# A two-block network on one core: diagonals, the values' bias, the state space preparation and weight conversions at other points of the program

## The chip, the cores and the metric

The kernel runs on one core of a Trainium2 chip, in one launch. The metric is the device time in microseconds (us). Five engines work at once, each through its own instructions in order: TensorE (PE in the rows), VectorE (DVE), ScalarE (ACT), GpSimd (POOL) and SyncE (SP), whose instructions here are the issues of transfers (DMA). An instruction waits for others by semaphores.

## The reference, cut to what matters

The network is two blocks of two layers each, on two streams of 256 tokens with 1024 features: the latent stream (LAT, x) and the context stream (CTX). All arithmetic is float32. Block 1:

```
for i in range(2):
    x  = ffn_half(x,  lat_m[0:3], ...)       # both streams: x + 0.5 * gate * swiglu(modulate(rmsnorm(x)))
    xc = ffn_half(xc, ctx_m[0:3], ...)
    h, hc = modulate(rmsnorm(x)), modulate(rmsnorm(xc))
    if i == 0:                               # convolution module, width 31, per channel, both streams
        y, yc = conv_module(h), conv_module(hc)
    else:                                    # neighbourhood attention; the context gives keys and values only
        qkv, qkvc = h @ na_w_qkv + na_b_qkv, hc @ na_w_qkv + na_b_qkv
        y = attention(q, k, v, kc, vc, rpb) @ na_w_o + na_b_o
    x = x + lat_m[5] * y
    x = ffn_half(x, lat_m[6:9], ...)         # and xc in layer 0
```

Block 2 starts from x and from a new context ctx_2; its first layer mixes by attention, its second by a state space scan:

```
a_re, a_im, bb_re, bb_im = s5_discretise(lam_re, lam_im, b_re, b_im, log_step)
y, h_end = s5_scan(u, a_re, a_im, bb_re, bb_im, c_re, c_im, h_re, h_im, emit)   # chunks of 128, two directions
```

The tables that the scan's matrix form needs (powers of a times bb and c, in several layouts) depend on weights alone, not on the streams.

## The kernel before, in words

**Products.** Every float32 product is made of three matmuls over a high part and a low part of each operand (hh and hl of the activations, wh and wl of the weights). Weights are loaded raw by SyncE (`_dma`, L164, three buffers), ScalarE copies the high part wh (L183) and VectorE subtracts to get the low part wl (L188), in `pump`. There are NBUF = 5 converted pieces at a time: when a piece is released, the next is converted.

**Stages.** They are marked f100 (feed-forward), conv, f102 (feed-forward), f110 (feed-forward), na (the neighbourhood attention), f112, and then block 2. A feed-forward stage (`ffn`) makes tiles of 128 hidden features over the 512 tokens of both streams (gu, 48 matmuls; the first n1 = 4 tiles stream by stage, each stream when its norm is ready), and then the down products (pd). Between two stages stands a norm: squares (sq, ScalarE) and their sums (acc, VectorE, L295), a column sum by TensorE (ssq), rv on VectorE (L266), rr on GpSimd (L268), a broadcast by TensorE (bc), then per tile nt (VectorE, L691), hh (ScalarE, L693) and hl (VectorE, L696). The next stage's first products wait for hh and hl.

**The convolution.** pj are the products of the pointwise layer; u comes from them by th and t (ScalarE). Eight channel tiles m follow, most taps on VectorE, some on TensorE by 128x128 diagonal matrices dgw, which ScalarE makes from the identity (L1004).

**The preparation.** `s5_pre` (the task `pre`) works on tables of the state space scan beside the feed-forward stages f100, f102 and f110, for indices d = 0 to 7. For each d GpSimd makes bb and its copy bbz (L2002 to L2007, L2062, L2063), vw (L2073 to L2085) and ow (L2110 to L2120), each twice (r = 1, then 0), and a rotation E in six doublings (L2153 to L2172). TensorE transposes vw (pvt) and multiplies ow with bbz (kp); ScalarE and VectorE copy the results to vt and kt; SyncE moves them through memory (dV, dO, dK, eight loads of tt and a dT, twice, and dE). Its tiles ow, vw, kt and tt have one buffer each. A task is a sequence of small steps; while it is started, one is put into the program whenever TensorE's modelled time has advanced by PRE_STEP. `stop` ends this at a stage's last group, and `drain`, behind f110, puts in all steps that are left.

**The attention's start.** In `na`, products for q, k and v of LAT and then of CTX run (pq, pk, pv); v gets its bias vb when it is copied out of the accumulators (vt, L1246), and vb is loaded in `values` (L1232), once for each group g of columns.

**What sets the order.** The program is written in one sequence, and a scheduler orders each engine's instructions by its own timeline, keeping the dependences. `behind_pe` adds a dependence without a wait, which holds an instruction behind the last matmul written so far in this order. On the chip each engine, SyncE too, goes through its instructions in the order so found.

Of the kernel before, what the change touches and what calls it, by code (L numbers as in the profile page):

```python
# [7 lines left out]
F32 = mybir.dt.float32  # L8
F32R = mybir.dt.float32r
AF = mybir.ActivationFunctionType  # L10
# [4 lines left out]
KT = 8  # L15
T = 256
FGROUPS = [(0, 6), (6, 8), (14, 8)]
NBUF = 5
# [59 lines left out]
class Core:  # L78
    def __init__(self, ctx, tc, ap):
        self.tc, self.nc, self.ap, self.es = tc, tc.nc, ap, ctx  # L80
        nc = tc.nc
        self.pe_t = 0.0
        self.n_mm, self.marks, self.pin = 0, [], None
        self.chains = []
        self.ticking = False
        self.tasks = []
        self.cv_behind = None
        P = lambda name, bufs, **kw: ctx.enter_context(tc.tile_pool(name=name, bufs=bufs, **kw))
        self.pool = lambda name, bufs=1, side="left": tc.tile_pool(name=name, bufs=bufs, side=side, reuse_waits="tile")
        self.const = P("const", 1)  # L90
        self.rawp = P("raw", NRAW)
        self.wp = P("w", NBUF)
        self.xp = P("xres", 1)
        self.hp = P("h", 1)
        self.sm = P("small", 3)
        self.tp = P("tmp", 3)
        self.psm = P("psm", 5, space=PSUM)
        self.psa = P("psa", 3, space=PSUM)
        self.chunks, self.pieces = [], []
        self.n_dma = self.n_cv = self.n_take = self.n_rel = 0  # L100
        self.dma_max, self.dma_behind = 1 << 30, False
        self.raw_t, self.cv_t, self.low_p = {}, {}, None

    def mark(self, name):
# [63 lines left out]
        self.n_dma += 1  # L168

    def pump(self):  # L170
        while self.n_cv < min(len(self.pieces), self.n_rel + NBUF):
            ci, off, n = self.pieces[self.n_cv]
            if ci >= self.dma_max:
                return
            while self.n_dma < min(len(self.chunks), ci + 1):
                self._dma()
            nc = self.nc
            r = self.raw_t[ci][:, off * 128:(off + n) * 128]
            hi = self.wp.tile([128, 8, 128], F32R, tag="wh", name="wh")
            lo = self.wp.tile([128, 8, 128], F32R, tag="wl", name="wl")  # L180
            h2 = hi[:, :n, :].rearrange("p k m -> p (k m)")
            l2 = lo[:, :n, :].rearrange("p k m -> p (k m)")
            ins = nc.scalar.activation(out=h2, in_=r, func=AF.Copy)  # L183
            if self.cv_behind:
                self.behind(ins, self.cv_behind)
            eng = nc.gpsimd if self.cv_behind else nc.vector
            self.low()
            self.low_p = lambda eng=eng, l2=l2, r=r, h2=h2: eng.tensor_sub(l2, r, h2.bitcast(F32))  # L188
            self.cv_t[self.n_cv] = (hi, lo)
            self.n_cv += 1  # L190
            last = self.n_cv == len(self.pieces) or self.pieces[self.n_cv][0] != ci
            if last:
                self.raw_t.pop(ci)
            while self.n_dma < min(len(self.chunks), ci + NRAW, self.dma_max):
                self._dma()
# [276 lines left out]
class Net(Core):  # L472
# [24 lines left out]

    def load_x(self, s, name):
        t = self.xp.tile([128, KT, T], F32, tag=f"x{s}", name=f"x{s}")
        self.nc.sync.dma_start(out=t, in_=self.ap[name])  # L500
        self.x[s] = t


    def load_c(self, names):
# [213 lines left out]
    def ffn(self, b, streams, ready, gate, after, nsplit=4, first=1, work=None, side=None, head=0, tail=0, begin=None):  # L718
# [5 lines left out]
        with ExitStack() as es:  # L724
# [12 lines left out]

            def background():
                nonlocal task
                if side is not None and not side.done:  # L740
                    self.start(side)
                if work is None:
                    return
                gen, n = work() if callable(work) else work
                task = Task(self, gen, (0.84 if two else 0.8) * (342e3 if two else 171e3) / n)
                self.start(task)
# [4 lines left out]
            def gu(ws, f0, c0, n, last=True, outer=None):  # L751
                glu(products(ws, c0, n, last, outer), f0, c0, n)
# [58 lines left out]
            for g, (f0, nf) in enumerate(FGROUPS):  # L811
                f = 0
                lastg = g == len(FGROUPS) - 1
                while f < nf:
                    if g == 0 and f == 0:
                        n1 = head + 2 if head else first
                        ws = {}
                        if begin:
                            with self.pool("room") as rp, tc.manual_schedule():
                                begin = begin([[rp.tile([128, 512], F32, name=f"room{i}{k}") for k in range(8)] for i in range(2)])  # L820
                                next(begin)
                                ws = [(self.take(), self.take()) for _ in range(first)]
                                ps = products(ws, 0, N, step=begin)
                                next(begin, None)
                            rooms()
                            glu(ps, 0, 0, N)
                            background()
                        for s in () if begin else streams:
                            order = list(range(n1)) if s == streams[0] else list(range(head, n1)) + list(range(head))
                            self.force(ready[s])  # L830
                            if not head:
                                ws = ws or [(self.take(), self.take()) for _ in range(first)]
                                gu(ws, 0, s * T, T, s == streams[-1])
                                continue
                            for i in order:
                                if i not in ws:
                                    ws[i] = (self.take(), self.take())
                                gu([ws[i]], i, s * T, T, s != streams[0] or i < head, i == order[0])
                                if i < head:
                                    ws.pop(i)  # L840
                        f += n1
                    else:
                        gu([(self.take(), self.take())], f, 0, N)
                        f += 1
                full = KT - nsplit if (lastg and two) else KT
# [115 lines left out]
    def conv(self, ready, gate, after, NPE=8, L=1, n_last=14):  # L961
# [3 lines left out]
        with self.pool("conv") as cp:  # L965
# [23 lines left out]
            def taps(m, ss, n_pe=NPE):  # L989
# [11 lines left out]
                dgs = diag.setdefault(m, [])  # L1001
                while len(dgs) < len(ek):
                    dg = cp.tile([128, 128], F32, tag="dgw", name="dgw", bufs=20)
                    nc.scalar.activation(out=dg, in_=self.ident, func=AF.Copy, scale=w(ek[len(dgs)]))  # L1004
                    dgs.append(dg)
                for i, k in enumerate(dk[2:]):
                    o = (vm, b2)[i % 2]
# [165 lines left out]
    def na(self, ready, gate, after, NR=1.1, NL=0.2):  # L1173
        nc, tc = self.nc, self.tc
        with self.pool("na") as np_, self.pool("na2", 2) as n2:
# [48 lines left out]
            new = lambda name: self.psm.tile([128, 512], F32, tag="m", name=name)  # L1224
            o_rhs = lambda k: self.h_rhs(k, 0, T)

            def produce():

                def values(g, ws, ts):
                    if g not in vb:  # L1230
                        vb[g] = n2.tile([128, T], F32, tag="vb", name="vb", bufs=1)
                        nc.sync.dma_start(out=vb[g], in_=self.ap["vbias"][g * T:(g + 1) * T].partition_broadcast(128))  # L1232
                        v_[g] = [n2.tile([128, 4, T], F32R, tag=f"v{x}", name=f"v{x}") for x in "hl"]
                    vh, vl = v_[g]
                    for t in ts:
                        ps = new("pv")
                        for k in range(KT):
                            wh, wl = [w.rearrange("p k m -> p (k m)")[:, (k % 4) * T:(k % 4 + 1) * T] for w in ws[k // 4]]
                            xh, xl = self.h_rhs(k, t * 128, 128)
                            self.mm(ps[:, :T], xh, wh, k == 0, False, 109)  # L1240
                            self.mm(ps[:, :T], xh, wl, False, False, 109)
                            self.mm(ps[:, :T], xl, wh, False, k == KT - 1, 109)
                            if k == 3:
                                yield
                        tmp = self.tp.tile([128, T], F32, tag="nt", name="vt")
                        nc.vector.tensor_add(tmp, ps[:, :T], vb[g])  # L1246
                        nc.scalar.activation(out=vh[:, t, :], in_=tmp, func=AF.Copy)
                        nc.vector.tensor_sub(vl[:, t, :], tmp, vh[:, t, :].bitcast(F32))
                        if t == 3:
                            vt[g] = (vh, vl)  # L1250
                        yield
# [5 lines left out]
                        yield  # L1257
                    q_out(m, ps)

                vb, v_ = {}, {}  # L1260

                wq, wk, *ws = [self.take() for _ in range(4)]
                wq1 = self.take()
# [51 lines left out]
                while done["pv"] < 16:  # L1315
                    yield
                split_o(7)
                for d, (w, ps) in enumerate(part):
                    self.gemm(ps[:, :T], w, o_rhs, [(7, 7)], False, True)
                    out(d, ps)  # L1320
                    self.release(1)
# [1110 lines left out]
    def network(self, out):  # L2432
# [79 lines left out]
        self.mark("na")  # L2512
        self.na(ready, gates(1, 1, 1, (LAT,)), lambda s, acc: norm(1, 1, 2, s, acc))

        self.load_x(CTX, "ctx_2")

        def ctx_norm():
            acc = self.new_acc(CTX)
# [89 lines left out]
```

## Time and profile before

| | us |
|---|---|
| median of 3 runs | 3609.77 (3609.4 to 3611.73) |
| profiled execution | 3612.36 |
| its span | 3610.5 |
| TensorE busy | 3482.7 |
| VectorE busy | 2590.3 |
| ScalarE busy | 1389.1 |
| GpSimd busy | 749.8 |

Matmuls overlap, and their ends are modelled, so busy time is not time at the peak. "Idle before" is the time an engine stood still just before an instruction, and behind the arrow stands what ended it. A stage's worth is read at its borders, where the engine at the end of the chain waits.

### The profile page before, as it was taken

What the parts mean: (1) busy time and instruction counts of PE and PEld (TensorE: products, weight loads), DVE (VectorE), ACT (ScalarE), POOL (GpSimd) and SP (SyncE); (2) the same over time, 40 slices, a digit from 0 to 9 for tenths busy, and PEclk for the clock granted to TensorE, in tenths of its full rate; (3) what the DMA queues carried; (4) which work ended last, traced back from release to release, by engine and by line L of the source; (5) the groups of instructions that cost most, each with busy time, mean ns of one, the idle gap of its engine ahead of it and who ended that gap; (6) DMA issues with size and microseconds to landing.
All of it is one profiled execution on the core that took longest, in us unless ns stands there. A gap on an engine that the chain in (4) does not pass through costs nothing.

```text
span 3610.5 us, 54700 instructions
## 1 busy us (share of the span) xinstructions
PE 3482.7 (96%) x21248; PEld 3056.4 (85%) x21248; DVE 2590.3 (72%) x4487; ACT 1389.1 (38%) x2428; POOL 749.8 (21%) x870
## 2 busy tenths in 40 slices
PE   8999998999999999999999999889999999999898
PEld 7888867888898888989998889779888988897898
DVE  8987697876586765768987766878887633368655
ACT  4222444422242323554443234655322432244443
POOL 5100001577657772000000001211000100014000
PEclk9999999999999999999999999999999999999899
DMA  7555211455454774236755542014557332238353
GB/s 260 200 189 197 71 59 48 162 190 186 164 169 170 257 242 138 92 120 235 262 187 188 182 145 97 34 50 153 208 206 247 134 124 94 102 120 300 121 197 119
DMA packets 157835, 579.35 MB, mean 160 GB/s; under 512 B 25220, under 2 KB 56708, under 8 KB 117896
## 3 DMA queue, kind: packets, MB, share of 16 engines
q1 hardware_dynamic: 157576, 575.86, 45.8%
q8 instruction: 167, 2.74, 0.3%
q14 instruction: 92, 0.75, 0.1%
HBM read 546.50 MB, written 29.29 MB: 159 GB/s over the span
## 4 chain that ended last, share of the span: by engine, by line
PE 89%; DVE 7%; ACT 2%; issue 1%; POOL 1%; DMA 0%; SPq 0%; POOLq 0%; DVEq 0%; ACTq 0%
PE gu L109 46%; PE pd L109 24%; PE pj L109 8%; PE po L109 2%; PE ptap L109 1%; PE pv L109 1%; PE pk L109 1%; PE ps L109 1%; DVE wl L188 1%; PE ssq L109 1%; PE pT L109 1%; PE pq L109 1%; PE bc L109 1%; DVE ry L2291 0%; DVE jk L612 0%
## 5 line engine op out<-in xcount | busy, mean ns | idle before, releaser
L183 ACT ACTIVATE wh<-raw 128x1024 fp32r<-128x1024 f32 (+1 forms) x679 | 700.8, 1038 | 1581.4 <-PE gu L109 911.7
L188 DVE TENSOR_TENSOR wl<-raw,wh 128x1024 fp32r<-128x1024 f32 (+1 forms) x677 | 839.3, 1244 | 358.5 <-ACT wh L183 348.2
L109 PE MATMUL gu<-hl,wh 128*128 128x512 f32 (+1 forms) x3136 | 1083.8, 347 | 5.6 <-DVE hl L696 4.6
L109 PE MATMUL gu<-hh,wh 128*128 128x512 f32 (+1 forms) x3136 | 1076.9, 348 | 10.0 <-ACT hh L693 6.2
L109 PE MATMUL gu<-hh,wl 128*128 128x512 f32 (+1 forms) x3136 | 1082.0, 346 | 0.0
L538 DVE CUSTOM_DVE_ANT_0 jk<-mw,cb,vec 128x1024 bf16<-128x1024 f32 x480 | 639.0, 1331 | 73.2 <-DMA mw<-in_mw_dram 68.4
L109 PEld LDWEIGHTS gu<-hl,wh 128*128 128x128 f32 x3136 | 600.7, 192 | 78.2 <-DVE hl L696 6.0
L109 PEld LDWEIGHTS gu<-hh,wh 128*128 128x128 f32 x3136 | 596.9, 192 | 81.6 <-ACT hh L693 7.6
L109 PEld LDWEIGHTS gu<-hh,wl 128*128 128x128 f32 x3136 | 600.7, 192 | 70.3 <-issue 1.0
L109 PE MATMUL pd<-Hl,wh 128*128 128x256 f32 (+1 forms) x1696 | 561.8, 332 | 0.0
L109 PE MATMUL pd<-Hh,wl 128*128 128x256 f32 (+1 forms) x1696 | 561.0, 332 | 0.0
L109 PE MATMUL pd<-Hh,wh 128*128 128x256 f32 (+1 forms) x1696 | 559.0, 331 | 0.0
L268 POOL TENSOR_TENSOR rr<-rv,mhalf 128x2 f32<-128x2 f32 (+1 forms) x34 | 28.9, 850 | 1852.9 <-DVE rv L266 1796.4
L109 PEld LDWEIGHTS pd<-Hl,wh 128*128 128x128 f32 x1696 | 322.0, 190 | 30.2 <-issue 0.4
L109 PEld LDWEIGHTS pd<-Hh,wl 128*128 128x128 f32 x1696 | 321.9, 190 | 30.2 <-issue 0.4
L109 PEld LDWEIGHTS pd<-Hh,wh 128*128 128x128 f32 x1696 | 321.5, 190 | 29.9
L779 DVE TENSOR_TENSOR gu<-sg,gu 128x512 f32<-128x512 f32 (+1 forms) x196 | 113.4, 579 | 192.6 <-PE gu L109 191.6
L109 PE MATMUL pj<-hh,wh 128*128 128x256 f32 (+1 forms) x736 | 226.3, 322 | 15.4 <-ACT hh L693 9.0
L109 PE MATMUL pj<-hl,wh 128*128 128x256 f32 (+1 forms) x736 | 231.2, 318 | 1.1 <-DVE hl L1089 1.0
L109 PE MATMUL pj<-hh,wl 128*128 128x256 f32 (+1 forms) x736 | 228.5, 316 | 1.1 <-DVE wl L188 1.1
L109 PEld LDWEIGHTS pj<-hh,wh 128*128 128x128 f32 x736 | 142.0, 200 | 25.8 <-ACT hh L693 9.9
L109 PEld LDWEIGHTS pj<-hl,wh 128*128 128x128 f32 x736 | 146.8, 200 | 9.0 <-issue 1.7
(425 smaller groups left out, 4332.1 us busy)
## 6 DMA issues: line engine op xcount, KB each, us to landing
raw<-in_gu_dram SPq DMA_DIRECT2D x186, 1024.0 KB, 4.9
mw<-in_mw_dram SPq DMA_DIRECT2D x280, 512.0 KB, 4.6
raw<-in_dn2b_dram SPq DMA_DIRECT2D x38, 1024.0 KB, 4.7
raw<-in_dn1b_dram SPq DMA_DIRECT2D x32, 1024.0 KB, 5.3
raw<-in_dn1a_dram SPq DMA_DIRECT2D x16, 768.0 KB, 4.4
raw<-in_pw_dram SPq DMA_DIRECT2D x12, 1024.0 KB, 4.7
raw<-in_dn2a_dram SPq DMA_DIRECT2D x16, 768.0 KB, 4.3
dO<-ow SPq DMA_DIRECT2D x32, 256.0 KB, 2.6
```

The lines of the kernel that those rows point to most:

```text
L109: ins = self.last_mm = self.nc.tensor.matmul(out=out, lhsT=lhsT, rhs=rhs, start=start, stop=stop, **kw)
L183: ins = nc.scalar.activation(out=h2, in_=r, func=AF.Copy)
L188: self.low_p = lambda eng=eng, l2=l2, r=r, h2=h2: eng.tensor_sub(l2, r, h2.bitcast(F32))
L268: nc.gpsimd.tensor_tensor(r[:, :ncol], v[:, :ncol], self.mhalf[:, :ncol], ALU.pow)
L538: self.behind_pe(nc.vector.tensor_tensor_reduce(out=jk, in0=tl[i], in1=self.cb[s], scale=1.0, scalar=self.V(f"mod_b{b}{l}")[:, j:j + 1], o ...
L779: nc.vector.tensor_mul(pr[:, :n], sg[:, :n], pu[:, :n])
```

## The change

Four things stand at other points of the program; no operation is added or removed.

- The diagonals dgw (now L1009) are held behind the last matmul written so far, by `behind_pe`.
- The preparation goes on in f102 and f110 not at the stage's start but at the second tile after the first n1 tiles. In f100 it starts as before.
- The load of the first vb is written at the head of `na`, ahead of the products, and the load of x for block 2's context (L500) is held behind the last matmul written so far.
- At the end of `na` a limit `cv_max` lets `pump` convert only what is left for the output projection and two pieces of f112, until f112's first norm is ready.

```
     def pump(self):
-        while self.n_cv < min(len(self.pieces), self.n_rel + NBUF):
+        while self.n_cv < min(len(self.pieces), self.n_rel + NBUF, self.cv_max):
...
             def background():
                 nonlocal task
-                if side is not None and not side.done:
+                if begin is not None and not side.done:
                     self.start(side)
...
                             self.force(ready[s])
+                            if self.cv_max < 1 << 30:
+                                self.cv_max = 1 << 30
+                                self.pump()
...
                     else:
+                        if g == 0 and f == n1 + 1 and side is not None and not side.done and side not in self.tasks:
+                            self.start(side)
                         gu([(self.take(), self.take())], f, 0, N)
...
-                    nc.scalar.activation(out=dg, in_=self.ident, func=AF.Copy, scale=w(ek[len(dgs)]))
+                    self.behind_pe(nc.scalar.activation(out=dg, in_=self.ident, func=AF.Copy, scale=w(ek[len(dgs)])))
...
+            vb = {}
+
+            def vbias(g):
+                vb[g] = n2.tile([128, T], F32, tag="vb", name="vb", bufs=1)
+                nc.sync.dma_start(out=vb[g], in_=self.ap["vbias"][g * T:(g + 1) * T].partition_broadcast(128))
+            vbias(0)
...
                 split_o(7)
+                self.cv_max = self.n_take + KT - 3 + 2
...
-        self.load_x(CTX, "ctx_2")
+        self.behind_pe(self.load_x(CTX, "ctx_2"))
```

The rows of the order below name tiles without their numbers where one is like another; numbers that stay tell buffers apart.

On ScalarE at the convolution's start, before (hh_96 to hh_100 are the tiles hh3 to hh7 of LAT):

```order
153 L693 ACTIVATE hh_95<-nt,mod_212 128x256
154 L285 ACTIVATE sq<-x_225 128x256
155 L183 ACTIVATE wh<-raw 128x1024
156 L1004 ACTIVATE dgw<-cst,vec 128x128 x17
157 L285 ACTIVATE sq<-x_225 128x256
158 L693 ACTIVATE hh_96<-nt,mod_212 128x256
159 L1004 ACTIVATE dgw<-cst,vec 128x128
160 L693 ACTIVATE hh_97<-nt,mod_212 128x256
161 L1004 ACTIVATE dgw<-cst,vec 128x128 x2
162 L693 ACTIVATE hh_98<-nt,mod_212 128x256
```

and after, from the same place, up to the first dgw:

```order
155 L183 ACTIVATE wh<-raw 128x1024
156 L285 ACTIVATE sq<-x_225 128x256
157 L693 ACTIVATE hh_96<-nt,mod_212 128x256
158 L693 ACTIVATE hh_97<-nt,mod_212 128x256
159 L693 ACTIVATE hh_98<-nt,mod_212 128x256
...
169 L693 ACTIVATE hh_99<-nt,mod_213 128x256
170 L985 ACTIVATE th<-pj,hb_3373 128x256
171 L693 ACTIVATE hh_100<-nt,mod_213 128x256
172 L1009 ACTIVATE dgw<-cst,vec 128x128 x8
173 L183 ACTIVATE wh<-raw 128x1024
```

The 20 dgw among the hh of LAT are gone from there; eight stand behind the last hh of CTX.

On GpSimd at the attention's start, before: the end of the last rotation E, and then rr of LAT, of CTX and of later norms in one row of six:

```order
651 L2166 TENSOR_TENSOR pt_11687<-E_12267 128x8x31
652 L2167 TENSOR_TENSOR E_12266<-pt_11686,pt_11687 128x8x31
653 L2170 TENSOR_TENSOR pt_11686<-E_12266,E_12267 128x8x31
654 L2171 TENSOR_TENSOR pt_11687<-E_12267,E_12266 128x8x31
655 L2172 TENSOR_TENSOR E_12267<-pt_11686,pt_11687 128x8x31
656 L268 TENSOR_TENSOR rr<-rv,mhalf 128x2 x6
```

and after, the stretch that ends with rr of CTX (ow_12576 and ow_12577 are ow of index 7, r = 0; E_12601 and E_12602 its rotation):

```order
611 L2127 TENSOR_TENSOR ow_12576<-ow_12576,ow_12578 128x576
612 L2166 MEMSET E_12601 128x8
613 L2169 COPY E_12601<-cc_1001 128x8
614 L2098 TENSOR_TENSOR vw_12554<-vw_12554,vw_12555 128x512
615 L2131 TENSOR_TENSOR ow_12578<-pw_12455,bc 128x576
616 L2178 TENSOR_TENSOR pt_12457<-E_12601 128x8
617 L2133 TENSOR_TENSOR ow_12577<-ow_12577,ow_12578 128x576
618 L2167 MEMSET E_12602 128x8
619 L2169 COPY E_12602<-cs_1002 128x8
620 L268 TENSOR_TENSOR rr<-rv,mhalf 128x2
621 L2179 TENSOR_TENSOR pt_12458<-E_12602 128x8
622 L2180 TENSOR_TENSOR E_12601<-pt_12457,pt_12458 128x8
```

The rr of LAT stands 84 instructions ahead of this one, and between them are the ow of index 6 (r = 0), its rotation E, and bb, bbz, both vw and both ow of index 7.

On SyncE up to the first vb, before (in front of these stand the four dE of index 7):

```order
390 L164 DMA raw<-in_naqk_dram 128x2048
391 L164 DMA raw<-in_nav_dram 128x2048
392 L2199 DMA dK_166<-kt 128x240
393 L2021 DMA tt<-dK_166 16x4x128 x8
394 L2023 DMA dT_174<-tt 128x512
395 L2021 DMA tt<-dK_166 16x4x128 x8
396 L164 DMA raw<-in_naqk_dram 128x2048
397 L2023 DMA dT_174<-tt 128x512
398 L500 DMA x_15165<-in_ctx_dram 128x2048
399 L1232 DMA vb<-in_vbias_dram 128x256
```

and after:

```order
367 L2212 DMA dK_166<-kt 128x240
368 L2034 DMA tt<-dK_166 16x4x128 x8
369 L2036 DMA dT_174<-tt 128x512
370 L2034 DMA tt<-dK_166 16x4x128 x6
371 L2193 DMA dE_157<-E_12601 128x256
372 L2193 DMA dE_158<-E_12601 128x256
373 L2034 DMA tt<-dK_166 16x4x128 x2
374 L2193 DMA dE_157<-E_12602 128x256
375 L2193 DMA dE_158<-E_12602 128x256
376 L2036 DMA dT_174<-tt 128x512
377 L164 DMA raw<-in_naqk_dram 128x2048
378 L1236 DMA vb<-in_vbias_dram 128x256
```

The load of x is gone from in front of vb, and the dE of index 7 have come in front of it.

## Rows read from the trace of the kernel before

**Rows 1.** The page, part 4: chain that ended last, by engine.

```profile
PE 89%; DVE 7%; ACT 2%; issue 1%; POOL 1%; DMA 0%; SPq 0%; POOLq 0%; DVEq 0%; ACTq 0%
```

**Rows 2.** Stretches: busy us of PE, PEld, DVE, ACT, POOL; granted clock; DMA; GB/s.

```profile
400.00:420.00 20.00, 15.70 (x114) 15.10 (x113) 15.77 (x36) 14.79 (x40) 0.70 (x1) 0.91 0.26 97
640.00:660.00 20.00, 13.36 (x75) 12.65 (x75) 19.79 (x26) 11.38 (x21) 16.69 (x18) 0.70 0.39 116
1040.00:1060.00 20.00, 18.00 (x143) 17.80 (x142) 20.00 (x25) 9.61 (x19) 18.41 (x11) 0.94 0.73 223
1620.00:1640.00 20.00, 13.11 (x82) 12.52 (x81) 15.41 (x33) 10.99 (x23) 0.70 (x1) 0.74 0.55 205
...
440.00:560.00 120.00, 120.00 (x487) 84.84 (x487) 117.24 (x182) 44.38 (x94) 0.00 (x0) 1.00 0.13 46
1412.40:1441.40 29.00, 22.25 (x180) 21.39 (x176) 18.48 (x42) 11.05 (x22) 0.87 (x1) 0.98 0.57 177
```

**Rows 3.** Timeline at the convolution's start: start, duration, engine, instruction [idle before].

```profile
406.02 5.07 ACT L1004 ACTIVATE dgw<-cst,vec 128x128 f32<-128x128 f32 x17
...
411.85 0.39 PE L109 MATMUL pj<-hh,wh 128*128 128x256 f32 x1 [4.25 <-ACT hh L693]
```

**Rows 4.** Timeline at f102's start, PE and DVE; last an hl elsewhere.

```profile
643.37 0.58 PE L109 MATMUL gu<-hl,wh 128*128 128x256 f32 x1 [2.51 <-DVE hl L696]
...
646.45 2.59 DVE L696 SCALAR_TENSOR_TENSOR hl<-nt,mod,hh 128x256 fp32r<-128x256 f32 x2
...
655.92 0.77 PE L109 MATMUL ssq<-invd,acc 128*128 128x1 f32 x3 [3.17 <-DVE acc L295]
...
1419.34 0.87 DVE L696 SCALAR_TENSOR_TENSOR hl<-nt,mod,hh 128x256 fp32r<-128x256 f32 x2
```

**Rows 5.** Group by line on GpSimd: busy, mean ns | idle before.

```profile
L2110 POOL TENSOR_TENSOR ow<-pw,bc 128x576 f32<-128x576 f32 x16 | 24.3, 1520 | 99.7 <-PE kp L109 99.5
```

**Rows 6.** Timeline of GpSimd, index 7 up to the norms.

```profile
1312.30 0.40 POOL L2002 TENSOR_TENSOR pt<-bc,cfr 128x128 f32<-128x128 f32 x1
...
1326.77 2.27 POOL L2085 TENSOR_TENSOR vw<-vw,vw 128x512 f32<-128x512 f32 x1
...
1345.25 1.06 POOL L2073 TENSOR_TENSOR vw<-pw,bb 128x512 f32<-128x512 f32 x1 [1.71 <-PE pvt L109]
...
1351.66 1.29 POOL L2085 TENSOR_TENSOR vw<-vw,vw 128x512 f32<-128x512 f32 x1
1362.21 1.17 POOL L2110 TENSOR_TENSOR ow<-pw,bc 128x576 f32<-128x576 f32 x1 [9.26 <-PE kp L109]
...
1367.23 2.29 POOL L2120 TENSOR_TENSOR ow<-ow,ow 128x576 f32<-128x576 f32 x1
1375.96 0.12 POOL L2153 MEMSET E<- 128x8 f32 x1 [6.45 <-PE pvt L109]
...
1395.21 0.79 POOL L2172 TENSOR_TENSOR E<-pt,pt 128x248 f32<-128x248 f32 x1
...
1419.50 0.87 POOL L268 TENSOR_TENSOR rr<-rv,mhalf 128x2 f32<-128x2 f32 x1 [13.72 <-DVE rv L266]
```

**Rows 7.** Timeline of TensorE at the attention's start.

```profile
1411.79 0.67 PE L109 MATMUL kp<-ow,bbz 128*32 128x128 f32 x16
...
1422.52 0.60 PE L109 MATMUL bc<-cst,rr 128*128 128x128 f32 x4
```

**Rows 8.** Timeline there: SyncE's queue (SPq), VectorE, TensorE.

```profile
1432.91 0.42 SPq L1232 DMA_DIRECT2D vb<-in_vbias_dram  x1
...
1440.98 0.42 DVE L1246 TENSOR_TENSOR vt<-pv,vb 128x256 f32<-128x256 f32 x1 [2.62 <-DMA vb<-in_vbias_dram]
...
1441.46 0.58 PE L109 MATMUL pv<-wh,hh 128*128 128x256 f32 x1 [5.10 <-DVE vt L1246]
```

**Rows 9.** Timeline at f112's start: VectorE and TensorE.

```profile
1614.35 1.22 DVE L188 TENSOR_TENSOR wl<-raw,wh 128x1024 fp32r<-128x1024 f32 x1 [3.04 <-ACT wh L183]
...
1629.04 1.02 PE L109 MATMUL ssq<-invd,acc 128*128 128x1 f32 x4 [4.75 <-DVE acc L295]
```

More of the change, by code (lines that the diff above doesn't have):

```diff
@@ L100, in __init__ @@
         self.n_dma = self.n_cv = self.n_take = self.n_rel = 0
-        self.dma_max, self.dma_behind = 1 << 30, False
+        self.dma_max, self.dma_behind, self.cv_max = 1 << 30, False, 1 << 30
         self.raw_t, self.cv_t, self.low_p = {}, {}, None
@@ L499, in load_x @@
         t = self.xp.tile([128, KT, T], F32, tag=f"x{s}", name=f"x{s}")
-        self.nc.sync.dma_start(out=t, in_=self.ap[name])
         self.x[s] = t
+        return self.nc.sync.dma_start(out=t, in_=self.ap[name])
     def load_c(self, names):
@@ L1230, in values @@
                     if g not in vb:
-                        vb[g] = n2.tile([128, T], F32, tag="vb", name="vb", bufs=1)
-                        nc.sync.dma_start(out=vb[g], in_=self.ap["vbias"][g * T:(g + 1) * T].partition_broadcast(128))
+                        vbias(g)
+                    if g not in v_:
                         v_[g] = [n2.tile([128, 4, T], F32R, tag=f"v{x}", name=f"v{x}") for x in "hl"]
@@ L1258, in query @@
                     q_out(m, ps)
-                vb, v_ = {}, {}
+                v_ = {}
                 wq, wk, *ws = [self.take() for _ in range(4)]
```

## The prediction

> **What bounds the kernel now.** I read the page's chain first, then the stretches at the stage borders, then single instructions there. TensorE carries 89% of the chain that ended last, VectorE 7%, GpSimd 1% [rows 1]. Outside the borders there is next to nothing to win, so every part of the change is priced at the border that it touches. Five borders matter, and each is a different wait [rows 2]: the convolution's start (TensorE busy 15.70 of 20 us), the start of f102 (13.36 of 20, granted clock 0.70), the start of f110 (18.00), the attention's start (22.25 of 29) and the start of f112 (13.11 of 20, clock 0.74).
>
> **Part 1, the diagonals.** Before the convolution ScalarE makes 17 dgw in a row, 5.07 us, between hh2 and hh3, and TensorE's first pj after them waits 4.25 us for hh [rows 3]. In the new order hh3 to hh7 and the next stream's hh go first, and 8 dgw follow. The tap stage behind it is VectorE's (117.24 of 120 us busy, ScalarE 44.38 [rows 2]): an earlier start moves it forward whole, and the dgw, made in ScalarE's gaps, are covered. I take the 4.25 us and 1.25 of the 1.8 us that the clock of 0.91 costs in those 20 us: minus 5.5. Bounds: 0, if VectorE's taps start by something else, and minus 6.0.
>
> **Part 2, the state space preparation's new start.** At f102's start GpSimd works 16.69 of 20 us [rows 2], and VectorE's operations beside it are longer: two hl took 2.59 us there and 0.87 where GpSimd was quiet [rows 4]. TensorE waits for those hl and for an acc: 2.51 and 3.17 us in the two large gaps [rows 4]. With GpSimd quiet, most of the stretch's 6.64 idle us goes, and part of what its clock of 0.70 costs [rows 2]: minus 7.5, bounds minus 2 (the acc chain stays late by itself) and minus 9. At f110's start the same reading gives the 2.00 idle us: minus 2, bounds 0 and minus 2.
>
> What is moved must still be done. The two later starts put the whole train (GpSimd, TensorE's pvt and kp, the copies, SyncE's dV, dO, dK, tt, dT, dE) back by five tiles each (n1 + 1). A tile is 48 matmuls over 512 columns, which I take as 96 over 256; 180 matmuls of the kernel's usual sort take 22.25 us [rows 2], so five tiles are some 59 us, twice. The train can't catch up: its buffers are single, and in front of GpSimd's ow alone it already stands idle for TensorE for 99.7 us in all [rows 5]. After f110 the program drains what is left. Before, that was one kp: it stands behind the last pd and ends at 1412.46 (call this K), and GpSimd had finished its last rotation at 1396.0 [rows 6, 7]. In the new order the kp behind the last pd is of index 6, so on GpSimd the rest of 6 and all of 7 stand behind K, and the second stream's rr stands behind all of that but the last rotation: 84 operations between the two rr, where there were none.
>
> The price by rows 6, as they ran for index 7 before:
> - three ow groups of five, 1362.21 to 1369.52 = 7.31 each: 21.9; two single ow products at 1.17: 2.3
> - one rotation E, 1375.96 to 1396.0: 20.0
> - bb, bbz and the first vw, 1312.30 to 1329.04 = 16.7, less two ow products in it (2.3): 14.4
> - the second vw group, 1345.25 to 1352.95 = 7.7, and one more product of 1.06: 8.8
>
> Sum 67.4 us as they ran. Some of these were held: the same vw addition took 2.27 us and 1.29 [rows 6]. My estimate is one such excess for each ow group, two for each vw, some 4 us in the bb stretch and 5 in the rotation: 12 in all, and 55 for the quiet chain. While it runs VectorE has little to do, since its next rv and hl wait for this very chain; so I stand near the quiet end, 58, and add 2 for the handovers to TensorE and back: rr at K+60 (bounds 55 and 69), against 1419.50 = K+7 before [rows 6]. TensorE's work of the first stream is over long before: from K to 1441.40 it had only 22.25 us of work for both streams [rows 2].
>
> The Trainium skill, "SBUF — State Buffer", section "Who interferes with whom", says that GpSimd and a VectorE instruction with two SBUF inputs exclude each other for whole instructions. The 2.59 against 0.87 us of rows 4 agree that one is held. By that rule a drain beside an idle VectorE would run at the 55 us end, and the total would come out 3 us lower; by the rows as they ran 9 higher.
>
> **Part 3, the values' bias.** Before, SyncE issues vb at 1432.91, right behind the load of x, VectorE's vt begins at 1440.98, and TensorE gets on at 1441.46 = K+29 after 5.10 us [rows 8]. The load of x now stands elsewhere, which alone would save that wait. But vb is still behind the last dT, and now behind the last dE too, and SyncE issues in order: dE needs the rotation E of index 7, which follows the rr. So: rr at K+60; the rest of that rotation 15.5 (bounds 14 and 18, from the 20.0 without its first operations, and without held ones); four issues of about 0.4 (vb's own 0.42): 1.6; landing and vt 7 (before 8.07, from 1432.91 to 1440.98; 3 at least, since there is no load of x ahead); 0.5 from vt to TensorE. TensorE resumes at K+84.6, where it resumed at K+29.0: **plus 55.6**, bounds plus 45 (55+14+1.6+3+0.5 = K+74) and plus 68 (K+97). What hides it: only those 22.25 us, used up on both sides. From rr to the second stream's bc took 3.0 us [rows 6, 7], and the 13.8 us of products between that bc and the wait (1422.52 to 1441.46, less 5.10) then end by about K+77, so vb is the last wait, if not by much. Behind the stalled TensorE stand the weight conversions, for lack of buffers; nothing in the attention gives the time back.
>
> **Part 4, the limit on conversions.** At f112's start ssq waits 4.75 us for acc [rows 9]; VectorE works through weight conversions of 1.22 us between the adds [rows 9], three fewer now (3.7 us). They come back while TensorE works on the first tiles. Minus 3 with the clock (0.74); bounds 0 (ScalarE's part or the adds set it) and minus 5.
>
> **Sum.** -5.5 - 7.5 - 2 - 3 + 55.6 = +37.6 us. The profiled execution took 3612.36 us, so 3650.0; it is 2.6 above the median of 3609.77 of the timed runs, so I predict 3647. Bounds: +45 - 22 = +23 and +68 - 2 = +66, that is 3633 to 3676.
>
> **Rivals.**
> (a) The drain is hidden, and it ends faster: GpSimd comes to the border with less behind K than the order suggests, or its operations run ahead of TensorE. For it: GpSimd has 1% of the chain before [rows 1]. Against: it waits for TensorE's kp and pvt by its single buffers [rows 5], and the order puts rr behind them. It decides from where TensorE resumes at K+47 (29 + 18); wholly hidden it gives 3610 - 18 = 3592.
> (b) The same stall, but GpSimd's operations run as long as in rows 6 (67 and 18), and the borders give back little: +68 - 8 = +60, 3670. For it: VectorE still copies kt and converts weights meanwhile; against: rows 4 show operations held only where both are busy.
> (c) vb isn't the last wait, since its small loads land quickly: then TensorE is late by the rr alone, K+63 at bc against 1422.52 = K+10, 53 us, less the 5.10 that vb cost before: 48 - 18 = +30, 3640.
>
> **How the numbers follow.** The forecast has 0.60, (b) 0.13, (c) 0.14, (a) 0.13, of which 0.09 full and 0.03 about even. A measurement of this kernel can tell 0.2%, 7 us, from no change. Slower by more than that: the forecast, (b), (c) and a rest of (a), 0.88; within it 0.03; faster 0.09. The range leaves out (a) and the far end of (b): 3622 to 3668; the likeliest case's own is 3635 to 3660.
>
> **What would show it.** After: pj without the 4.25 us gap at the convolution's start; VectorE's hl at f102's start at about 0.43 us each; rr of the attention's second stream some 50 us or more behind the first, with rotations and ow, vw between; TensorE nearly idle for over 50 us before the second stream's products; vb issued right behind dE and dT. I am wrong if the two rr stand within 25 us of each other, or if the attention's start is no longer than before.

## The result and the profile after

The changed kernel takes 3634.82 us (median of 4 runs, 3632.36 to 3639.12), the kernel before 3609.76; the ratio is 1.0068, with an interval of 1.0056 to 1.0081. It is slower by 25 us, where 37 were forecast (3647, range 3622 to 3668). The profiled execution took 3634.27 us, its span is 3632.5. That is 22 us above the profiled execution before (3612.36), which ran 2.6 us over its median; so the traces show 22 us where the timed medians show 25.

The chain that ended last, by engine, answers to [rows 1]:

```profile
PE 86%; DVE 7%; POOL 3%; issue 2%; ACT 1%; DMA 0%; SPq 0%; POOLq 0%; DVEq 0%; ACTq 0%
```

GpSimd's share has grown from 1% to 3%. The stretches show where. They answer to [rows 2], with the same columns, and each window is moved about as far as the first rr of its stage moved (the table below has these shifts). The fourth runs from the end of the kp behind the last pd to the end of the stall, the fifth is the start of f112:

```profile
400.00:420.00 20.00, 18.43 (x128) 17.34 (x127) 16.91 (x40) 10.75 (x22) 0.73 (x2) 0.91 0.25 100
638.00:658.00 20.00, 18.90 (x146) 18.90 (x146) 17.92 (x37) 13.34 (x26) 1.54 (x1) 0.91 0.50 186
1026.00:1046.00 20.00, 20.00 (x169) 20.00 (x169) 20.00 (x35) 11.13 (x22) 8.87 (x5) 1.00 0.56 185
1391.50:1473.00 81.50, 39.78 (x275) 34.79 (x273) 25.62 (x46) 15.83 (x32) 69.26 (x120) 0.68 0.41 127
1648.80:1668.80 20.00, 13.09 (x83) 12.51 (x82) 15.46 (x34) 11.04 (x23) 0.71 (x1) 0.74 0.68 259
```

The start of f102 is nearly full now (18.90 of 20, before 13.36) and that of f110 full (20.00, before 18.00); f112's is as it was (13.09, before 13.11). At f102's start GpSimd works 1.54 us, and the two hl that took 2.59 us there [rows 4] take 0.89:

```profile
640.87 0.89 DVE L696 SCALAR_TENSOR_TENSOR hl<-nt,mod,hh 128x256 fp32r<-128x256 f32 x2
```

The attention's start has become a stretch of 81.5 us in which GpSimd works 69.26 and TensorE 39.78; TensorE's granted clock in it is 0.68.

GpSimd in that stretch (start, duration, instruction, idle before), from the first stream's rr to the second's and to the end of the last rotation; this answers to [rows 6]:

```profile
1384.14 0.71 POOL L268 TENSOR_TENSOR rr<-rv,mhalf 128x2 f32<-128x2 f32 x1 [26.87 <-DVE rv L266]
1391.66 1.68 POOL L2123 TENSOR_TENSOR ow<-pw,bc 128x576 f32<-128x576 f32 x1 [6.81 <-PE kp L109]
...
1446.40 1.41 POOL L2133 TENSOR_TENSOR ow<-ow,ow 128x576 f32<-128x576 f32 x1
...
1448.13 0.71 POOL L268 TENSOR_TENSOR rr<-rv,mhalf 128x2 f32<-128x2 f32 x1
...
1464.10 0.72 POOL L2185 TENSOR_TENSOR E<-pt,pt 128x248 f32<-128x248 f32 x1
```

The two rr are 64.0 us apart (before 14.4), and the second waits for nothing but the instructions in front of it: no bracket stands behind it. From the first ow on GpSimd nowhere pauses for more than 0.14 us, so the drain is GpSimd's own work and waits for no other engine. Before, GpSimd had waited 13.72 us for the second rr's input [rows 6].

TensorE there, answering to [rows 7, 8]:

```profile
1390.87 0.67 PE L109 MATMUL kp<-ow,bbz 128*32 128x128 f32 x16
...
1432.48 1.11 PE L109 MATMUL pvt<-cst,vw 128*128 128x128 f32 x4 [24.24 <-POOL vw L2090]
...
1445.22 1.11 PE L109 MATMUL pvt<-cst,vw 128*128 128x128 f32 x4 [4.89 <-POOL vw L2098]
...
1451.23 0.58 PE L109 MATMUL pk<-hh,wh 128*128 128x256 f32 x1 [1.11 <-ACT hh L693]
...
1463.79 0.36 PE L109 MATMUL pv<-wh,hh 128*128 128x256 f32 x1 [2.85 <-DVE kl L1202]
...
1473.00 0.79 PE L109 MATMUL pk<-hh,wh 128*128 128x512 f32 x1 [5.00 <-DVE vt L1258]
```

K, the end of the kp, is at 1391.54, 20.9 us earlier than before. TensorE then meets the preparation's transposes, which wait for GpSimd's vw, and resumes for good at 1473.00 = K+81.5, where it resumed at K+29.0. Its last transposes get their vw only at 1445.22, 2.9 us before the second rr. So two things hold the second stream's products back: the rr in GpSimd's queue, and these transposes, which stand in front of the products in TensorE's own order. No run here moves the rr alone. SyncE's queue and VectorE give the last wait:

```profile
1464.85 0.81 SPq L2193 DMA_DIRECT2D dE<-E  x2
1465.83 0.33 SPq L2036 DMA_DIRECT2D dT<-tt  x1
1466.20 0.44 SPq L164 DMA_DIRECT2D raw<-in_naqk_dram  x1
1466.69 0.44 SPq L1236 DMA_DIRECT2D vb<-in_vbias_dram  x1
...
1472.52 0.42 DVE L1258 TENSOR_TENSOR vt<-pv,vb 128x256 f32<-128x256 f32 x1 [8.88 <-DMA vb<-in_vbias_dram]
```

The last dE goes out when the rotation has ended (1464.82), and vb behind it.

Each norm has its rr on GpSimd, in the same sequence in every kernel, and these serve as milestones. The table gives how much later each comes than in the profile before (us, minus is earlier), for the changed kernel and for the experiments below. "First" and "second" are the two streams; the second rr of f102 lies behind both large gaps of [rows 4]; "end" is the last rr, at 3600.3 before.

| kernel | f102, first (630.7) | f102, second (658.5) | f110, first (1022.1) | attention, first (1405.1) | attention, second (1419.5) | f112 (1630.3) | 2492.9 | end |
|---|---|---|---|---|---|---|---|---|
| changed | -2.0 | -10.7 | -14.1 | -20.9 | +28.6 | +28.8 | +29.7 | +21.9 |
| 1 late only | +1.4 | -7.1 | -10.7 | -17.5 | +32.0 | +32.7 | +33.2 | +25.0 |
| 2 without late | -3.7 | -4.8 | -3.1 | -1.4 | -1.4 | -0.8 | +1.9 | -6.7 |
| 3 all, 1200 | -1.7 | -10.4 | -10.9 | -10.3 | -10.3 | -12.0 | -10.2 | -16.0 |
| 4 late in f110 | +0.6 | +0.6 | +0.6 | -3.8 | +5.4 | +10.3 | +11.7 | +7.0 |
| 5 limit only | -1.6 | -1.6 | -2.8 | +1.1 | +1.1 | -2.4 | -2.9 | -3.8 |
| 6 diagonals only | -2.6 | -3.8 | -2.0 | -1.4 | -1.4 | -4.5 | -6.2 | -16.0 |
| 7 bias and x only | +0.1 | +0.1 | +0.1 | +0.1 | +0.1 | -0.9 | -0.9 | -7.3 |
| 8 all, vb elsewhere | -1.7 | -10.4 | -13.9 | -20.7 | +28.8 | +24.7 | +26.9 | +21.4 |
| 9 1200 only | +0.7 | +0.7 | +2.2 | +5.8 | +5.0 | +3.9 | +3.7 | -4.5 |
| 10 late, 1200 | +1.0 | -7.6 | -8.3 | -7.2 | -7.2 | -9.2 | -7.7 | -13.2 |
| 11 all, 1250 | -3.5 | -12.0 | -8.1 | -12.5 | -9.5 | -6.2 | -4.7 | -9.9 |

So the 22 us of the profile are: 20.9 won up to the attention, 49.7 lost between there and f112, and 6.9 won behind it, in block 2.

### The profile page after: what moved, and what is told of

It reads as the page before. It is cut to its first block, busy times and chain, and to the rows that moved or that the text cites. A ratio compares the mean times of both kernels' runs of the same rounds, so it can differ in the third digit from the quotient of the medians.

```text
span 3632.5 us, 54687 instructions
## 1 busy us (share of the span) xinstructions
PE 3481.5 (96%) x21248; PEld 3053.3 (84%) x21248; DVE 2570.5 (71%) x4487; ACT 1387.4 (38%) x2428; POOL 730.9 (20%) x870
## 4 chain that ended last, share of the span: by engine, by line
PE 86%; DVE 7%; POOL 3%; issue 2%; ACT 1%; DMA 0%; SPq 0%; POOLq 0%; DVEq 0%; ACTq 0%
PE gu L109 46%; PE pd L109 23%; PE pj L109 8%; PE po L109 2%; PE ptap L109 1%; PE pk L109 1%; PE ps L109 1%; PE pv L109 1%; DVE wl L188 1%; PE ssq L109 1%; PE pT L109 1%; PE bc L109 1%; PE pq L109 0%; DVE tl L1601 0%; DVE ry L2304 0%
```

## The experiments

Theory A: the tail of the preparation, pushed behind f110, makes the whole loss. Rivals are named in the expectations. All times are medians, ratios are to runs of the kernel before on the same chip.

**1. Part 2 alone** on the kernel before:

```
-                if side is not None and not side.done:
+                if begin is not None and not side.done:
...
+                        if g == 0 and f == n1 + 1 and side is not None and not side.done and side not in self.tasks:
+                            self.start(side)
```

> Only part 2 on the kernel before (the state space preparation goes on later in f102 and f110); diagonals, bias, x and conversions as before. Theory A (the preparation's tail stands behind f110 and in front of the attention's second rr): 3637 us (3625 to 3645), and the two rr of the attention's start some 60 us apart. Rival B (the loss comes from the moved loads of vb and x or from the limit on conversions, and the later start costs nothing): 3590 to 3600 us, rr 15 us apart.

Measured 3637.51 us, ratio 1.0074 (1.0057 to 1.0091). Part 2 alone makes the loss, and the rr of the attention are 64 us apart (14.4 before, and 49.5 more by the table). Rival B falls.

**2. Parts 1, 3 and 4 without part 2.**

```
-                        if g == 0 and f == n1 + 1 and side is not None and not side.done and side not in self.tasks:
-                            self.start(side)
...
-                if begin is not None and not side.done:
+                if side is not None and not side.done:
```

> Parts 1, 3 and 4 without part 2. Theory A: no stall; the 5.1 us wait for vb goes and the convolution starts 2 to 5 us earlier: 3597 to 3604 us. Rival B: the attention's start stays long: 3625 us or more. Rival C (small shifts of order in block 2 are worth as much as the parts): anywhere in 3595 to 3612, with the differences behind f112.

Measured 3603.84 us, ratio 0.9982 (0.9973 to 0.9992): 6 us faster than before. But at f112 it is level (-0.8), and the gain stands in block 2. Of these parts only the load of x reaches into block 2, and the gain there is no smaller in experiment 6, which leaves that load alone. A's stall is gone, but the 6 us are of C's kind.

**3. The whole change with closer steps.**

```
-PRE_STEP = 1500
+PRE_STEP = 1200
```

> The whole change, with PRE_STEP 1200 in place of 1500: the preparation's steps come closer together, and by the order of GpSimd none stands between or behind the two rr of the attention. Theory A (the tail alone makes the loss; the earlier arrival at the attention, 20.9 us, is mostly quiet borders): 3580 to 3595 us. Rival D (the 20.9 us are mostly work that was pushed out of f102 and f110 into the stall, and comes back when it is done there): 3597 to 3606 us. Rival B: 3625 us or more.

Measured 3593.87 us, ratio 0.9953 (0.9938 to 0.9968). With no instruction of the preparation left between or behind the two rr, 41 us of the changed kernel's time are gone, and it beats both kernels. GpSimd's rr and the resuming TensorE in it:

```profile
1394.73 0.71 POOL L268 TENSOR_TENSOR rr<-rv,mhalf 128x2 f32<-128x2 f32 x1 [8.24 <-DVE rv L266]
1409.17 0.87 POOL L268 TENSOR_TENSOR rr<-rv,mhalf 128x2 f32<-128x2 f32 x1 [13.72 <-DVE rv L266]
```

```profile
1428.21 0.39 PE L109 MATMUL pv<-wh,hh 128*128 128x256 f32 x1 [2.18 <-DVE vt L1258]
```

The two rr are 14.4 us apart again, with the same 13.72 us wait as before. The time lies in A's range, though some 4 us of it come behind f112. This kernel is 10.3 us early at the attention, the changed kernel 20.9. Up to f102's second rr the two agree (-10.4 and -10.7); from there on the changed kernel wins 10.3 us more and this one nothing. So half of the changed kernel's lead was work only deferred (rival D's point), and the other half stands up to f102's second rr (A's quiet borders, and the diagonals).

**4. Late in f110 only.**

```
+        self.stage = name
...
-                if side is not None and not side.done:
+                if side is not None and not side.done and self.stage != "f110":
...
+                        if g == 0 and f == n1 + 1 and side is not None and not side.done and side not in self.tasks:
+                            self.start(side)
```

> The kernel before with the preparation late in f110 alone; in GpSimd's order 16 of its instructions stand between the two rr of the attention and 34 behind, in place of 84 and 35. Theory A: a stall in proportion to what stands between, plus the wait for vb behind the last dE: 10 to 25 us lost there, 2 to 7 won in f110: 3612 to 3630 us. Rival B: 3602 to 3608 us.

Measured 3618.38 us, ratio 1.0024 (1.0015 to 1.0033). The rr are 23.7 us apart, vb goes out at 1447.76, and TensorE waits 6.27 us for vt. From the first rr to f112 it loses 14.1 us; f110 gives 4.4. That is A again, with a smaller tail.

**5. The limit on conversions alone** (part 4).

```
-        while self.n_cv < min(len(self.pieces), self.n_rel + NBUF):
+        while self.n_cv < min(len(self.pieces), self.n_rel + NBUF, self.cv_max):
...
+                self.cv_max = self.n_take + KT - 3 + 2
```

> Part 4 alone on the kernel before. On all five engines the order of instructions is that of the kernel before, word for word. Theory E (the limit never binds, so part 4 does nothing): 3610 us within 0.2%, eight weight conversions again between the adds at f112's start, the 4.75 us wait unchanged; its trace then shows how far two profiles of one program differ from stage to stage. The prediction's term: 3607 us, the wait 2 to 3 us shorter.

Measured 3609.19 us, ratio 1.0003 (0.9993 to 1.0014). Theory E holds: every engine's order is that of the kernel before, so the part does nothing. In the changed kernel too the wait at f112's start is what it was [rows 9]:

```profile
1657.88 0.37 PE L109 MATMUL ssq<-invd,acc 128*128 128x1 f32 x1 [4.76 <-DVE acc L295]
```

Its row in the table is also a measure of noise: two profiles of one order differ by up to 4 us at a milestone.

**6. The diagonals alone** (part 1).

```
-                    nc.scalar.activation(out=dg, in_=self.ident, func=AF.Copy, scale=w(ek[len(dgs)]))
+                    self.behind_pe(nc.scalar.activation(out=dg, in_=self.ident, func=AF.Copy, scale=w(ek[len(dgs)])))
```

> Part 1 alone on the kernel before. The prediction's term: 5.5 us won, 3604 us. Rival F (the taps' start waits for weight pieces that TensorE releases, and what is won at the first pj is lost again by then; only the order behind the taps changes): 3606 to 3610 us, with the first tap of VectorE within 0.5 us of where it was.

Measured 3597.96 us, ratio 0.9974 (0.9963 to 0.9985), more than either theory said: both missed. The table puts only 2.6 us of its profile's 16.0 in front of f102, and 11.5 behind f112. The traces show where the 4.25 us of [rows 3] went (the first row TensorE, then ScalarE, then VectorE's first tap). In this experiment:

```profile
409.15 0.50 PE L109 MATMUL pj<-hh,wh 128*128 128x256 f32 x2 [0.30 <-ACT hh L693]
...
410.86 0.61 PE L109 MATMUL ssq<-invd,acc 128*128 128x1 f32 x4 [1.20 <-DVE acc L295]
...
424.78 1.06 ACT L183 ACTIVATE wh<-raw 128x1024 fp32r<-128x1024 f32 x1 [1.66 <-PE pj L109]
...
429.69 0.75 DVE L1008 SCALAR_TENSOR_TENSOR v<-u,vec,v 128x512 f32<-128x512 f32 x1 [0.94 <-ACT v L997]
```

In the changed kernel:

```profile
408.45 0.39 PE L109 MATMUL pj<-hh,wh 128*128 128x256 f32 x1 [0.32 <-ACT hh L693]
...
425.59 1.06 ACT L183 ACTIVATE wh<-raw 128x1024 fp32r<-128x1024 f32 x1 [1.65 <-PE pj L109]
...
430.50 0.75 DVE L1013 SCALAR_TENSOR_TENSOR v<-u,vec,v 128x512 f32<-128x512 f32 x1 [0.94 <-ACT v L1002]
```

and the kernel before:

```profile
425.74 1.06 ACT L183 ACTIVATE wh<-raw 128x1024 fp32r<-128x1024 f32 x1 [3.28 <-PE pj L109]
...
430.65 0.75 DVE L1008 SCALAR_TENSOR_TENSOR v<-u,vec,v 128x512 f32<-128x512 f32 x1 [0.94 <-ACT v L997]
```

In the changed kernel the first pj starts 3.4 us earlier, but the weight piece that TensorE's pj releases, and with it the first tap, only 0.15. In this experiment it is 2.7 us for pj and 0.96 for the first tap, outside the 0.5 that rival F allowed. So most of what is won at pj is lost again by the taps, as F says, but not all. Part of the loss is a new wait behind pj, 1.20 us of ssq for acc, which the changed kernel has too; the rest wasn't isolated. By the table the six kernels with part 1 reach f102 1.7 to 3.7 us early, the six without it between 1.6 early and 1.4 late; the means lie 2.9 us apart.

**7. Bias and x alone** (part 3).

```
+            vbias(0)
...
-        self.load_x(CTX, "ctx_2")
+        self.behind_pe(self.load_x(CTX, "ctx_2"))
```

> Part 3 alone (vb written earlier, the load of x held back). The prediction's reading of the 5.1 us wait for vb: about 5 us won if x in front of it was the cause, 3605 us. Rival G (vb still waits for the last dT in SyncE's order, so half of the wait stays or another takes its place): 3607 to 3611 us.

Measured 3602.95 us, ratio 0.9982 (0.9973 to 0.9992). The time is below both ranges. At the attention it goes as G said: the wait for vt falls from 5.10 to 2.05 us, and others of 2.12 and 0.53 us follow it at the first pT; at f112 the profile is 0.9 us ahead, within the noise. The 6 us come in block 2 again, and the rows show one place where the two differ, around the norms at 2848 and 2869. GpSimd's rr and TensorE, before:

```profile
2848.07 0.70 POOL L268 TENSOR_TENSOR rr<-rv,mhalf 128x2 f32<-128x2 f32 x1 [5.79 <-DVE rv L266]
2869.38 0.71 POOL L268 TENSOR_TENSOR rr<-rv,mhalf 128x2 f32<-128x2 f32 x1 [6.41 <-DVE rv L258]
...
2874.12 0.74 PE L109 MATMUL gu<-hh,wh 128*128 128x256 f32 x4 [0.83 <-ACT hh L693]
```

and in this experiment, where TensorE has no such wait for hh:

```profile
2845.81 0.69 POOL L268 TENSOR_TENSOR rr<-rv,mhalf 128x2 f32<-128x2 f32 x1 [5.40 <-DVE rv L266]
2863.70 0.71 POOL L268 TENSOR_TENSOR rr<-rv,mhalf 128x2 f32<-128x2 f32 x1 [8.00 <-PE gu L109]
```

The rr are 21.3 us apart before and 17.9 here, with 173 and 151 matmuls of TensorE between them: the order is another. The distance is as short in the changed kernel (17.9), and shorter than before in all experiments that have another order, but not in the fifth, which has the order of before (22.7). VectorE and ScalarE have another order around this place in the changed kernel and in every experiment but the fifth: the scheduler orders block 2 by a timeline that edits ahead of it shift. The wait of 0.83 us is only a part of the 6 us, and where the rest comes from wasn't worked out. The parts don't add up either: alone, part 1 wins 11 us and part 3 wins 6, but parts 1, 3 and 4 together win 6 (experiment 2).

**8. The whole change, vb from ScalarE's queue.**

```
-                nc.sync.dma_start(out=vb[g], in_=self.ap["vbias"][g * T:(g + 1) * T].partition_broadcast(128))
+                (nc.sync if g else nc.scalar).dma_start(out=vb[g], in_=self.ap["vbias"][g * T:(g + 1) * T].partition_broadcast(128))
```

> The whole change, with the first vb issued from ScalarE's queue instead of SyncE's, so that it doesn't stand behind dT and dE of index 7; it comes behind the second stream's last hh there. If vb is the last wait of the attention's start by as much as TensorE's 5.00 us gap in the changed kernel shows: 3627 to 3632 us (3634.8 less 5, a little less if another wait follows). If the second stream's rr decides alone: 3633 to 3637 us.

Measured 3633.71 us, ratio 1.0071 (1.0056 to 1.0086): not told apart from the changed kernel as a time, and in the range said for an rr that decides alone. vb goes out at 1463.9, and within the stage this kernel is 4.1 us ahead of the changed one at f112, about as much as two profiles of one order differ by (experiment 5). TensorE's 5.00 us wait for vt is gone, and one for kl has grown from 2.85 us:

```profile
1465.90 0.55 PE L109 MATMUL pv<-wh,hh 128*128 128x256 f32 x1 [4.87 <-DVE kl L1202]
```

So vb is the last wait in the changed kernel's trace, but with it out of the way the next one takes over most of its time: it is worth 4 us at most, and the timed runs show none of it. The chain in front of the second rr, and the transposes beside it, make the rest.

**9. Closer steps alone**, on the kernel before, as a control for experiment 3.

```
-PRE_STEP = 1500
+PRE_STEP = 1200
```

> Control for the third experiment: the kernel before with PRE_STEP 1200 alone, nothing of the change. Theory A (the closer steps only keep the tail out of the attention): the borders of the kernel before stay, and some 4 to 8 us may go in block 2, as with every edit that shifts the order there: 3600 to 3610 us. Rival H (the closer steps by themselves make that experiment's gain): 3590 to 3597 us.

Measured 3611.00 us, ratio 1.0005 (0.9996 to 1.0014), a little over the end of A's span: the closer steps win nothing by themselves. Rival H falls. Up to the attention this kernel loses 5.1 us behind f102's first rr, and f110 has waits of TensorE that the kernel before lacks, the longest 2.77 us of a pvt for vw; its profile wins this back in block 2.

**10. Part 2 with closer steps**, on the kernel before.

```
-PRE_STEP = 1500
+PRE_STEP = 1200
...
-                if side is not None and not side.done:
+                if begin is not None and not side.done:
...
+                        if g == 0 and f == n1 + 1 and side is not None and not side.done and side not in self.tasks:
+                            self.start(side)
```

> Part 2 alone with PRE_STEP 1200: late in f102 and f110, but with nothing left for the attention. Theory A: f102's start is won (8 to 10 us by the second rr there), nothing is lost at the attention, block 2 gives some 4 to 8 us: 3592 to 3602 us. If a later start costs by itself, without a tail: 3610 us or more.

Measured 3596.57 us, ratio 0.9961 (0.9947 to 0.9975). Against experiment 1 only the steps differ, and 41 us lie between them: a late start is a gain as long as the train arrives. Its place is f102's start: between the two rr there this kernel wins 8.6 us.

**11. A shorter tail**: the whole change with steps between the two.

```
-PRE_STEP = 1500
+PRE_STEP = 1250
```

> The whole change with PRE_STEP 1250: 28 of the preparation's instructions stand between the two rr of the attention and 12 behind them (84 and 35 with 1500, none with 1200). Theory A: a stall in proportion, by the 14 us that 16 and 34 instructions cost and the 50 us of 84 and 35: 10 to 20 us on the 3593.9 of the kernel with 1200, so 3603 to 3616 us. Rival B: 3590 to 3598 us.

Measured 3606.93 us, ratio 0.9992 (0.9983 to 1.0002), as A said of the time. A's way to it, a stall in proportion to the instructions, doesn't hold: the rr are 17.4 us apart with 28 instructions between, against 23.7 with the 16 of experiment 4, and from the first rr to f112 6.3 us are lost against 14.1. vb goes out at 1425.79, 1447.76 and 1466.69 in experiments 11, 4 and the changed kernel, and their times come in that order.

## Why the prediction was right, and where its sizes were off

**The stall (parts 2 and 3): right in place and nearly in size.** Forecast plus 55.6 us at TensorE's resuming, measured K+81.5 against K+29.0: 52.5. Its pieces, forecast and measured: rr at K+60, 56.6 (1448.13); the rest of the rotation 15.5, 16.7 (1448.13 to 1464.82); the issues up to vb 1.6, 1.9; landing and vt 7, 5.8; to TensorE 0.5, 0.5. Of the 52.5 the milestones keep 49.7 at f112. The reading of the drain as a nearly quiet chain was right: 56.6 stands near the 55 of unheld operations, not at 67, and the 2 us for handovers weren't needed. The ow addition that took 2.29 us [rows 6] took 1.41 there, beside a VectorE that worked 25.62 of 81.5 us; single operations were still long (an ow product of 2.15 us, others 1.15 to 1.4). The Trainium skill, "SBUF — State Buffer", section "Who interferes with whom", says that a VectorE instruction with two SBUF inputs contends with a GpSimd instruction that reads SBUF. These times agree with that; no run here shows the lock itself.

The prediction named the rr and vb as what TensorE waits for. It left out that TensorE meets the tail's transposes first, in its own order. The last of them get their vw 2.9 us ahead of the rr, so the sum didn't suffer.

**f102 and f110: the borders were right, but deferred work was left out.** Forecast 7.5 and 2, measured 12.1 and 6.8 by the milestones. The border of f102 was read rightly: between its two rr 8.7 us are won, and 8.5 to 8.7 in every kernel that starts late in f102, against at most 1.1 in the others. Two hl of VectorE took 0.89 us there, as forecast. The other 10.3 us up to the attention the prediction put at nothing beyond f110's 2. They appear in the three kernels with the full tail (10.3 to 10.4), in part in experiment 4 with its smaller one (4.4), hardly in experiment 11 (0.5), and not at all in experiments 3 and 10, where the train arrives. So they are work of the preparation that these stages did before and that is now done in the stall: before, TensorE made no pvt or kp behind K, after it made 24 and 48, and the copies and GpSimd's operations went with them. f110's wait of 2.00 us went as forecast, but no milestone shows it as a gain of its own.

**The diagonals: the cause of the gap was right, the carrying over was wrong.** The gap at pj went (4.25 to 0.32 us), but of the forecast 5.5 us 2.0 are left at f102, and 2.9 on the mean over the kernels with and without this part. The step that failed is that an earlier start moves the tap stage forward whole: before the first tap stands a weight piece that waits for TensorE's pj (1.65 us in the changed kernel), and the first tap came only 0.15 to 0.96 us earlier in the two traces shown.

**The limit on conversions: wrong.** Forecast 3 us, measured nothing. The step took it that the limit leaves three conversions fewer there. It doesn't bind: the same eight conversions stand between the adds in the changed kernel as before, and ssq waits 4.76 us.

**Left out altogether: block 2.** 6.9 us of the profile are won there, by an order that most of these edits give.

**What of the sum was luck.** The gains up to the attention come to 20.9 us where the whole of the gains was forecast as 18. That they are so close is luck: the deferred work, left out, made up for the diagonals and the limit, which were too large. The trace has 49.7 - 20.9 - 6.9 = 21.9 us in place of the forecast's 37.6. Of the 15.7 between them, block 2 makes 6.9, the gains 2.9, the stall's size 3.1, and 2.8 are what the stall has lost by f112.

**Rivals.** (a), a hidden drain, falls with experiment 1. (b), held operations, falls with the 56.6 us. (c), that vb isn't last, is wrong by the trace: VectorE waits 8.88 us for vb last. It is wrong by little, for with vb out of the way the next wait takes over (experiment 8).

## What to carry to other kernels

Before you start background work later, count what of it is then left at its deadline: here the same later start is 28 us slower with a tail behind the deadline and 13 us faster with steps close enough to leave none (some 4 of the 13 come behind f112). Look for the tail in the order of every engine that carries both the background work and a step of the critical chain: here a 0.7 us rr behind 84 instructions on GpSimd, and the next products behind the tail's transposes on TensorE. Where a scheduler orders the program by a timeline, an edit also reorders what comes long after it, so compare stage by stage, and take a control that changes nothing in the stage you price.

## What was not expected of the hardware

Two profiles of the same order differ by up to 4 us at a milestone (experiment 5), about as much as the smaller terms of the prediction; timed runs of the kernel before spread from 3605.43 to 3615.72 us. During the drain TensorE's granted clock was 0.68 over 81.5 us, and four pvt, which took 0.60 us at the drain's start (1395.08), took 1.11 us behind the gap of 24.24 us. That didn't lengthen the drain, since GpSimd never waited for them.
